# The loads of the first down products' activations move from the sync queue to GpSimd's queue

## The chip, the cores and the metric

The kernel runs on one core of a Trainium2 chip. The metric is the device time of one execution in microseconds (us). Engines are named as in the profile: PE is TensorE's matmuls, PEld its weight loads, DVE is VectorE, ACT is ScalarE, POOL is GpSimd, SP is SyncE, which here does nothing but issue DMAs.

## The reference

One step of one layer of a hybrid decoder, for 1024 prompt tokens and 8 sampled ones. A mixer (an HGRN2 and a Mamba-2 branch) comes first; the change touches only the feed-forward part at the end:

```python
h2 = _rmsnorm(x, p['norm_mlp']) * (1 + sc2) + sh2
x = x + g2 * (jnp.square(jax.nn.relu(h2 @ p['w_up'])) @ p['w_down'])
...
y_prompt = _rmsnorm(xp, norm_final)
y_sample = _rmsnorm(xs, norm_final)
```

D_MODEL is 1024 and the inner width is 4096. Everything is float32.

## The kernel before

Activations lie transposed: a **plane** is 128 channels by NT = 1032 tokens (1024 + 8). The model width is 8 planes, the inner width 32. A float32 product is made of three fp32r matmuls: every operand is split into hi (a copy rounded to fp32r, by ACT) and lo (the rest, by DVE), and the sum takes hi*lo, lo*hi and hi*hi. A block of weights is 128x1024 (512 KB); `load_w` (L46) loads it on SP (L51), makes `wh` on ACT (L53) and `wl` on DVE (L55). There are three buffers for the raw weights `wr`, and two each for `wh` and `wl`, so a load of weights waits in SP's queue until an earlier block has been split.

**Up products.** `phase_ffn` (L1137) makes 32 planes of `relu(up)^2`. They do not stay on the core: each is written to a DRAM tile `ad0` to `ad31`, in pieces, by stores in GpSimd's queue (L1148). Planes 6 to 31 come in pairs by a Strassen scheme, `strassen_pair` (L1095): seven products (1, 7, 6, 2, 5, 4, 3 in this order) of two halves q each, every one an accumulation of 12 matmuls at L1122, and 8 pieces of result per pair, each 128x258. A piece goes through one of four buffers `r`; two of the pieces are evacuated by ACT (L1151) and DVE (L1152), the other six by DVE alone (L1177, L1178), partly with sums that ACT has kept (L1111).

**Down products.** The 32 planes are read back in four chunks c of 8, by `load_split_in` (L856): a DMA from `ad` into the tile of `lo` (L862), `hi` on ACT (L863), `lo` in place on DVE (L864). For a chunk, the 8 output planes m are made one after the other from 8 activations and one block of weights `w_down`. The first of them, chunk 0 with m = 0, is made by `DenseK` (L99, matmuls at L114): it takes the activations one plane at a time as they arrive, 9 matmuls each (three spans s of 344 tokens by three products), so plane 7 can only follow planes 0 to 6. All other products (L86) take all 8 planes of a chunk in one go. Chunk 0 thus is planes 0 to 7, from `ad0` to `ad7`; chunk 1 is planes 8 to 15, from `ad8` to `ad15`, which is not needed until the 8 products of chunk 0 are done.

**What sets the order.** The order on each engine is the scheduler's, made when the kernel is built, from priorities: what stands in `high_priority(AHEAD)` is drawn forward, and that holds for the loads of weights, for the evacuations and for the loads of chunk 0. On an engine or in a DMA queue nothing overtakes: an instruction that waits holds those behind it. A load of a plane waits for its two buffers: those of planes 0 to 3 are freed by product 1 of the last Strassen pair, 4 to 7 by its product 5, those of chunk 1 by its products 4 and 3.

The lines and names used below: `wr_23450`, `wr_23582`, `wr_23674`, `wr_23766`, `wr_23858` are the first five blocks of `w_down`, called w0 to w4; the eight stores of the last pair are called s1 to s8 in their order.

Of the kernel before, what the change touches and what calls it, by code (L numbers as in the profile page):

```python
# [23 lines left out]
KD = 8  # L24
# [13 lines left out]
def cs(s):  # L38
    return slice(s * SW, (s + 1) * SW)
# [6 lines left out]
def load_w(k, src, prio=AHEAD):  # L46

    nc = k.nc
    with k.tc.high_priority(prio):
        wr = stage(k)[:, :KD * P]  # L50
        nc.sync.dma_start(wr, src)  # L51
        wh = k.wp.tile([P, KD * P], F32R, tag="wh", name="wh", bufs=2)
        nc.scalar.activation(wh, wr, AF.Copy)  # L53
        wl = k.wp.tile([P, KD * P], F32R, tag="wl", name="wl", bufs=2)
        nc.vector.tensor_tensor(wl, wr, wh.bitcast(F32), op=ALU.subtract)  # L55
    return wh, wl
# [21 lines left out]
def dense_split(k, w, X, s, evac, M=P):  # L78
    wh, wl = w
    nc = k.nc  # L80
    acc = k.ps.tile([P, 512], F32, tag="acc", name="acc", bufs=3)
    n = len(X)
    for i, (xh, xl) in enumerate(X):
        sl = slice(i * M, (i + 1) * M)
        for j, (a, b) in enumerate(((wh, xl), (wl, xh), (wh, xh))):
            last = nc.tensor.matmul(acc[:M, :SW], a[:, sl], b[:, cs(s)],  # L86
                                    start=(i == 0 and j == 0), stop=(i == n - 1 and j == 2))
    with k.tc.high_priority(AHEAD):
        evac(s, acc[:M, :SW])
    return last  # L90


def dense(k, src, X, evac):

    w = load_w(k, src)
    return [dense_split(k, w, X, s, evac) for s in range(NS)]
# [756 lines left out]
    return split_plane(k, r, tag)  # L853


def load_split_in(k, src, tag):  # L856

    nc = k.nc
    hi = k.pp.tile([P, NT], F32R, tag=tag, name="hi")
    lo = k.pp.tile([P, NT], F32R, tag=tag, name="lo")  # L860
    raw = lo.bitcast(F32)
    nc.sync.dma_start(raw, src)  # L862
    nc.scalar.activation(hi, raw, AF.Copy)  # L863
    nc.vector.tensor_tensor(lo, raw, hi.bitcast(F32), op=ALU.subtract)  # L864
    return hi, lo
# [86 lines left out]
def gated_add(k, s, dst, base, ps, gate):  # L952

    nc = k.nc
    n = SW if s < NS - 1 else SW - NB
    nc.vector.scalar_tensor_tensor(dst[:, :n], ps[:, :n], gate[:, 0:1], base[:, :n], ALU.mult, ALU.add)  # L956
    if n < SW:
        t = k.sp.tile([P, NB], F32, tag="ga", name="ga", bufs=2)
        nc.vector.tensor_tensor(t, ps[:, n:], gate[:, 1:9], op=ALU.mult)
        nc.vector.tensor_tensor(dst[:, n:], t, base[:, n:], op=ALU.add)  # L960


def sum_sq(k, acc, x, first):
    nc = k.nc
    if first:
        nc.scalar.activation(acc, x, AF.Square)
        return
    t = k.sp.tile([P, SW], F32, tag="sq", name="sq", bufs=2)
    nc.scalar.activation(t, x, AF.Square)
    nc.vector.tensor_tensor(acc, acc, t, op=ALU.add)  # L970


def rstd_model(k, acc):
    nc = k.nc
    ps = rec_ps(k, "ss")
    nc.tensor.matmul(ps[:, :SW], k.ones, acc, start=True, stop=True)
    return rstd_from(k, ps[:, :SW], SW, 1.0 / 1024)
# [45 lines left out]
def strassen_planes(k, h2, T, i):  # L1023

    nc = k.nc
    a, b = stage(k), stage(k)  # L1030
    for x, (xh, xl) in ((a, h2[i]), (b, h2[i + 4])):
        nc.vector.tensor_tensor(x, xh.bitcast(F32), xl.bitcast(F32), op=ALU.add)
    (b11, b12), (b21, b22) = [(x[:, :HN], x[:, HN:]) for x in (a, b)]

    def sub(out, x, y):
        nc.vector.tensor_tensor(out, x, y, op=ALU.subtract)
    sub(b11, b12, b11)
    sub(b12, b22, b12)
    sub(b22, b22, b11)
    sub(b21, b21, b22)  # L1040
    for x, tag, ts in ((a, "A", (1, 3)), (b, "Q3", (4, 2))):
        p = split_plane(k, x, tag, "th", "tl")
        for n, t in enumerate(ts):
            T[t].append(tuple(y[:, n * HN:(n + 1) * HN] for y in p))


def strassen_operands(h2, T):

    def quarter(r, c):
        return [tuple(p[:, c * HN:(c + 1) * HN] for p in h2[4 * r + i]) for i in range(KD // 2)]  # L1050
    return {1: quarter(0, 0), 2: quarter(1, 0), 3: quarter(1, 1), 4: T[4], 5: T[1], 6: T[2], 7: T[3]}
# [85 lines left out]
def phase_ffn(k, x1, h2):  # L1137
    nc = k.nc
    NF = 4 * KD
    up = k.i["w_up"]  # L1140
    ad = [k.dp.tile([P, NT], F32, name="ad%d" % j) for j in range(NF)]
    bufs = iter(range(1 << 20))

    def out(j, cols):
        n = next(bufs) % 4
        pool, tag = (k.sp2, "mt") if n < 2 else (k.sp, "sq")
        r = pool.tile([P, SW], F32, tag=tag, name="r", bufs=2)[:, :cols.stop - cols.start]
        return r, lambda: nc.gpsimd.dma_start(ad[j][:, cols], r)  # L1148

    def relu2(r, ps):  # L1150
        nc.scalar.activation(r, ps, AF.Relu)  # L1151
        nc.vector.tensor_tensor(r, r, r, op=ALU.mult)  # L1152

    def evac_up(j):
        def f(s, ps):
            r, store = out(j, cs(s))
            relu2(r, ps)
            store()
        return f

    ws = [load_w(k, up[j]) for j in range(2)]
    for j, s in [(j, s) for j in range(2) for s in LAST[:2]] + [(0, LAST[2]), (1, LAST[2])]:
        dense_split(k, ws[j], h2, s, evac_up(j))

    T = {n: [] for n in (1, 2, 3, 4)}
    for j in range(2, 6):
        dense(k, up[j], h2, evac_up(j))
        strassen_planes(k, h2, T, j - 2)
    X = strassen_operands(h2, T)
    for n in range(6, NF, 2):  # L1170
        def evac(m, half, q, a, ps, n=n):
            c = half * HN + q * HQ
            r, store = out(n + m, slice(c, c + HQ))
            if a is None:
                relu2(r, ps)
            else:
                nc.vector.tensor_tensor(r, a, ps, op=ALU.add)  # L1177
                nc.vector.scalar_tensor_tensor(r, r, 0.0, r, ALU.max, ALU.mult)  # L1178
            store()
        strassen_pair(k, (up[n], up[n + 1]), X, evac)  # L1180

    def add(m):
        return lambda s, ps: gated_add(k, s, x1[m][:, cs(s)], x1[m][:, cs(s)], ps, k.modT[:, 40 + m, :])

    def act(c, j):
        tag = "A" if c % 2 == 0 else "Q2" if j < 4 else "Q3"
        return load_split_in(k, ad[c * KD + j], tag)
    down = k.i["w_down"]
    aX = []
    d = DenseK(k, (down[0],), (add(0),))  # L1190
    for j in range(KD):
        with k.tc.high_priority(AHEAD):
            aX.append(act(0, j))
        d.step(*aX[j])
    for c in range(4):
        nX = []
        for m in range(KD):
            if c == 3:
                break
            if c or m:  # L1200
                dense(k, down[c * KD + m], aX, add(m))
            nX.append(act(c + 1, m))
        if c < 3:
            aX = nX
    for s in LAST:
        acc = k.sp2.tile([P, SW], F32, tag="sqa", name="sqa", bufs=1)
        for m in range(KD):
            w = load_w(k, down[3 * KD + m])
            dense_split(k, w, aX, s, add(m))
            sum_sq(k, acc, x1[m][:, cs(s)], m == 0)  # L1210
        y = rstd_model(k, acc)
        for m in range(KD):
            xx = x1[m][:, cs(s)]
            nc.vector.scalar_tensor_tensor(xx, xx, k.norm_final[:, m:m + 1], y, ALU.mult, ALU.mult)
            nc.sync.dma_start(k.o["y"][m][:, cs(s)], xx)
# [175 lines left out]
```

## Time and profile before

| | |
|---|---|
| Median of 3 runs | 2525.54 us (2525.27 to 2528.78) |
| The profiled execution's own time | 2526.23 us |
| Its span, first to last instruction | 2524.5 us |
| Around the span | 1.73 us |
| SP's queue (q1) | 279.99 MB |
| GpSimd's queue (q0) | 17.57 MB |

Times inside the execution are counted from the start of the span. The last Strassen pair's matmuls end at about 2137.4, the first down product follows at 2137.45, and the products of chunk 0 run until about 2237. In a timeline row the columns are: start, length, engine, line, operation, out<-in, shape, count of merged instructions, and in brackets the engine's idle time ahead of the row and what ended it. A row with a count above one gives the start of the first and the time to the end of the last. A row of the stretches has its bounds, its length, the busy time of each engine, the granted clock of PE, the busy share of the 16 DMA engines, and the GB/s that they moved.

### The profile page before, as it was taken

The page shows a single profiled execution, that of the slowest core. Times are in us where ns is not written, and L with a number is a line of the kernel's source. Part 1 is how long each engine was busy: PE and PEld are TensorE (multiplying, and loading weights), DVE is VectorE, ACT ScalarE, POOL GpSimd, SP SyncE. Part 2 cuts the span into 40 slices and gives each one's busy share as a digit, 9 for nine tenths or more (in the row PEclk, how much of TensorE's full clock was granted, in tenths as well). Part 3 has the DMA queues.
Part 4 walks back from the last instruction along what each step waited for, and adds up shares of the span by engine and source line. Part 5 has one row for each costly group of instructions (what it writes and reads, how often), then busy time and mean ns, then how long its engine had stood idle before and what let it go on. Part 6 is the DMA issues. An engine that isn't in the chain of part 4 may idle for free.

```text
span 2524.5 us, 47612 instructions
## 1 busy us (share of the span) xinstructions
PE 2479.3 (98%) x19822; PEld 2419.3 (96%) x19822; DVE 1755.6 (70%) x3513; ACT 1068.9 (42%) x1577; POOL 70.0 (3%) x138
## 2 busy tenths in 40 slices
PE   8999999999999999999999999999999999999998
PEld 7999999999999999999999999999999999999997
DVE  7788888888677687787887844366976666443356
ACT  4455555555444544535535533123533334221123
POOL 0000000000000000000000000000012222000000
PEclk9999999999999999999999999999999999999999
DMA  6323232223333243343343554224333325332134
GB/s 257 120 101 103 102 102 101 93 99 93 103 111 130 91 145 122 99 145 121 101 152 106 186 193 143 76 101 136 99 112 104 106 101 183 111 110 92 68 104 148
DMA packets 103256, 300.96 MB, mean 119 GB/s; under 512 B 19056, under 2 KB 26032, under 8 KB 103024
## 3 DMA queue, kind: packets, MB, share of 16 engines
q1 hardware_dynamic: 96352, 279.99, 33.3%
q0 software_dynamic: 6256, 17.57, 2.0%
q8 instruction: 156, 2.56, 0.4%
q14 instruction: 60, 0.49, 0.1%
q10 hardware_dynamic: 432, 0.35, 0.0%
HBM read 241.02 MB, written 57.10 MB: 118 GB/s over the span
## 4 chain that ended last, share of the span: by engine, by line
PE 72%; issue 11%; DVE 9%; ACT 3%; POOL 2%; DMA 2%; SPq 0%; POOLq 0%; DVEq 0%; ACTq 0%
PE acc L86 60%; POOL ad L1148 2%; PE acc L114 2%; PE y_ps L807 1%; DVE wl L55 1%; PE yi_ps L811 1%; PE kvx_ps L771 1%; DVE lv L554 1%; DVE lv L549 1%; DMA st<-sth 1%; PE xt_ps L759 1%; PE cb_ps L741 1%; ACT lv L551 1%; DVE lv L552 1%; ACT wh L53 0%
## 5 line engine op out<-in xcount | busy, mean ns | idle before, releaser
L86 PE MATMUL acc<-hl,wh 128*128 128x344 f32 x2232 | 722.4, 324 | 0.0
L86 PE MATMUL acc<-hh,wl 128*128 128x344 f32 x2232 | 721.9, 323 | 0.2 <-DVE wl L55 0.2
L86 PE MATMUL acc<-hh,wh 128*128 128x344 f32 x2232 | 716.7, 321 | 0.0
L86 PEld LDWEIGHTS acc<-hl,wh 128*128 128x128 f32 x2232 | 419.6, 188 | 3.7 <-issue 0.8
L86 PEld LDWEIGHTS acc<-hh,wl 128*128 128x128 f32 x2232 | 419.7, 188 | 3.0 <-issue 1.8
L86 PEld LDWEIGHTS acc<-hh,wh 128*128 128x128 f32 x2232 | 420.6, 188 | 1.4 <-issue 0.4
L86 PE MATMUL acc<-hi,wl 128*128 128x344 f32 x1224 | 392.4, 321 | 1.3 <-DVE wl L55 1.3
L86 PE MATMUL acc<-lo,wh 128*128 128x344 f32 x1224 | 391.7, 321 | 1.4 <-ACT wh L53 1.4
L86 PE MATMUL acc<-hi,wh 128*128 128x344 f32 x1224 | 391.1, 320 | 0.0
L53 ACT ACTIVATE wh<-wr 128x1024 fp32r<-128x1024 f32 x198 | 209.0, 1056 | 381.2 <-PE acc L86 306.0
L55 DVE TENSOR_TENSOR wl<-wr,wh 128x1024 fp32r<-128x1024 f32 x198 | 242.3, 1224 | 182.4 <-ACT wh L53 180.4
L86 PEld LDWEIGHTS acc<-lo,wh 128*128 128x128 f32 x1224 | 230.5, 188 | 2.0 <-ACT wh L53 2.0
L86 PEld LDWEIGHTS acc<-hi,wl 128*128 128x128 f32 x1224 | 230.2, 188 | 2.1 <-DVE wl L55 1.9
L86 PEld LDWEIGHTS acc<-hi,wh 128*128 128x128 f32 x1224 | 230.3, 188 | 0.2
L956 DVE SCALAR_TENSOR_TENSOR x<-acc,modT,x 128x344 f32<-128x344 f32 (+1 forms) x120 | 68.7, 572 | 189.2 <-PE acc L86 188.4
L691 DVE SCALAR_TENSOR_TENSOR cv<-raw,cst,cv 128x1024 f32<-128x1024 f32 x96 | 122.9, 1280 | 0.0
L1122 PE MATMUL b<-th,wl 128*128 128x258 f32 x416 | 117.7, 283 | 0.0
L1122 PE MATMUL b<-tl,wh 128*128 128x258 f32 x416 | 117.7, 283 | 0.0
L1122 PE MATMUL b<-th,wh 128*128 128x258 f32 x416 | 117.5, 282 | 0.0
L1148 POOL DMA_DIRECT2D ad<-r x122 | 65.8, 540 | 1468.4 <-DVE nrm_t L146 1204.2
L551 ACT ACTIVATE lv<-lv 128x1280 f32<-128x1280 f32 x48 | 61.0, 1273 | 85.7 <-DVE lv L549 83.4
L683 ACT ACTIVATE raw<-acc 128x344 f32<-128x344 f32 x96 | 42.9, 455 | 120.1 <-PE acc L86 119.3
(287 smaller groups left out, 4458.4 us busy)
## 6 DMA issues: line engine op xcount, KB each, us to landing
wr<-w_ssm SPq DMA_DIRECT2D x48, 512.0 KB
wr<-w_down SPq DMA_DIRECT2D x48, 512.0 KB
wr<-w_ada SPq DMA_DIRECT2D x36, 512.0 KB
lo<-ad SPq DMA_DIRECT2D x32, 516.0 KB
wr<-w_hg SPq DMA_DIRECT2D x32, 512.0 KB
w<-cumd SPq DMA_DIRECT2D x32, 512.0 KB
wr<-w_up SPq DMA_DIRECT2D x32, 512.0 KB
ad<-r POOLq DMA_DIRECT2D x104, 129.0 KB, 2.2
```

What stands on the lines that cost most here:

```text
L53: nc.scalar.activation(wh, wr, AF.Copy)
L55: nc.vector.tensor_tensor(wl, wr, wh.bitcast(F32), op=ALU.subtract)
L86: last = nc.tensor.matmul(acc[:M, :SW], a[:, sl], b[:, cs(s)], start=(i == 0 and j == 0), stop=(i == n - 1 and j == 2))
L114: k.nc.tensor.matmul(ac[s][:, :SW], a[:, sl], b[:, cs(s)], start=(i == 0 and j == 0), stop=(i == self.n - 1 and j == 2))
L549: nc.vector.tensor_tensor(EQ[:, :, off:off + n], b4[:, :, lo:], b4[:, :, lo - 1:lo].broadcast_to([P, nb, n]), op=ALU.subtract)
L551: nc.scalar.activation(E, E, AF.Exp)
L552: nc.vector.tensor_tensor(EK, EK, kk[:, sl], op=ALU.mult)
L683: dense(k, w, k.hX, lambda s, ps: nc.scalar.activation(raw[:, 3 + s * SW:3 + (s + 1) * SW], ps, AF.Copy))
L691: nc.vector.scalar_tensor_tensor(cv[:, :T], raw[:, j:j + T], cw[:, j:j + 1], cv[:, :T], ALU.mult, ALU.add)
L956: nc.vector.scalar_tensor_tensor(dst[:, :n], ps[:, :n], gate[:, 0:1], base[:, :n], ALU.mult, ALU.add)
L1122: nc.tensor.matmul(acc, a[:, sl], x[:, cols], start=(p in (1, 7, 2) and i == 0 and j == 0), stop=(i == KD // 2 - 1 and j == 2), skip_group ...
L1148: return r, lambda: nc.gpsimd.dma_start(ad[j][:, cols], r)
```

## The change

`load_split_in` gets a queue as an argument, and the eight loads of chunk 0 are issued by GpSimd; those of chunks 1 to 3 stay with SP.

```diff
-def load_split_in(k, src, tag):
+def load_split_in(k, src, tag, queue=None):
...
-    nc.sync.dma_start(raw, src)
+    (queue or nc.sync).dma_start(raw, src)
...
     def act(c, j):
         tag = "A" if c % 2 == 0 else "Q2" if j < 4 else "Q3"
-        return load_split_in(k, ad[c * KD + j], tag)
+
+        return load_split_in(k, ad[c * KD + j], tag, nc.gpsimd if c == 0 else None)
```

The scheduler places things anew around it, on SP, POOL, ACT and DVE. PE's order is unchanged.

SP's queue before, from the load of plane 3 to that of plane 7. The tile on the right says which plane it is: `ad3` is plane 3, `ad10` plane 10.

```order
L862 DMA lo_23502<-ad3_19627 128x1032
L51 DMA wr_23674<-w_down 128x1024
L862 DMA lo_23516<-ad4_19628 128x1032
L862 DMA lo_23762<-ad10_19634 128x1032
L862 DMA lo_23578<-ad8_19632 128x1032
L862 DMA lo_23530<-ad5_19629 128x1032
L51 DMA wr_23766<-w_down 128x1024
L51 DMA wr_23858<-w_down 128x1024
L862 DMA lo_23544<-ad6_19630 128x1032
L862 DMA lo_23670<-ad9_19633 128x1032
L862 DMA lo_23854<-ad11_19635 128x1032
L862 DMA lo_23558<-ad7_19631 128x1032
```

The same place now, from w2 (`wr_23674`) to the last load of chunk 1:

```order
L51 DMA wr_23674<-w_down 128x1024
L862 DMA lo_23762<-ad10_19634 128x1032
L862 DMA lo_24038<-ad13_19637 128x1032
L862 DMA lo_23578<-ad8_19632 128x1032
L51 DMA wr_23766<-w_down 128x1024
L862 DMA lo_23854<-ad11_19635 128x1032
L862 DMA lo_24130<-ad14_19638 128x1032
L51 DMA wr_23858<-w_down 128x1024
L862 DMA lo_23670<-ad9_19633 128x1032
L862 DMA lo_23946<-ad12_19636 128x1032
L862 DMA lo_24222<-ad15_19639 128x1032
```

Planes 0 to 7 are gone from the queue. Planes 13 and 14 of chunk 1 have moved ahead of plane 9, and all of chunk 1 still shares the queue with the weights w3 and w4.

POOL's queue at the end of the up products as it is now. The L1148 rows are the stores s2 to s8 of the last pair, which stood there before too, in the same order and with nothing between them. (The loads of planes 0 to 2 now stand ahead of s1, and s1 ahead of the first row.)

```order
L862 DMA lo_23502<-ad3_19627 128x1032
L1148 DMA ad30_19654<-r_23350 128x258
L1148 DMA ad31_19655<-r_23366 128x258
L862 DMA lo_23516<-ad4_19628 128x1032
L1148 DMA ad31_19655<-r_23382 128x258
L1148 DMA ad31_19655<-r_23398 128x258
L862 DMA lo_23530<-ad5_19629 128x1032
L1148 DMA ad31_19655<-r_23414 128x258
L1148 DMA ad30_19654<-r_23430 128x258
L1148 DMA ad30_19654<-r_23446 128x258
L862 DMA lo_23544<-ad6_19630 128x1032
L862 DMA lo_23558<-ad7_19631 128x1032
```

Each load now stands among the stores: plane 3 behind s1, plane 4 behind s3, plane 5 behind s5, planes 6 and 7 behind s8.

ACT before, from the hi of plane 4 to the hi of plane 7. The hi tiles of planes 4 to 7 are 23515, 23529, 23543 and 23557; of planes 8 to 11 23577, 23669, 23761 and 23853; of planes 12 to 15 23945, 24037, 24129 and 24221. `r_23446` is the evacuation of s8, `wh_23584` is the split of w1.

```order
L863 ACTIVATE hi_23515<-lo_23516 128x1032
L1151 ACTIVATE r_23446<-b1_23233 128x258
L53 ACTIVATE wh_23584<-wr_23582 128x1024
L863 ACTIVATE hi_23761<-lo_23762 128x1032
L863 ACTIVATE hi_23577<-lo_23578 128x1032
L863 ACTIVATE hi_23529<-lo_23530 128x1032
L863 ACTIVATE hi_23543<-lo_23544 128x1032
L863 ACTIVATE hi_23669<-lo_23670 128x1032
L863 ACTIVATE hi_23853<-lo_23854 128x1032
L863 ACTIVATE hi_23557<-lo_23558 128x1032
```

The same place now:

```order
L863 ACTIVATE hi_23515<-lo_23516 128x1032
L863 ACTIVATE hi_23761<-lo_23762 128x1032
L1151 ACTIVATE r_23446<-b1_23233 128x258
L53 ACTIVATE wh_23584<-wr_23582 128x1024
L863 ACTIVATE hi_24037<-lo_24038 128x1032
L863 ACTIVATE hi_23529<-lo_23530 128x1032
L863 ACTIVATE hi_23577<-lo_23578 128x1032
L863 ACTIVATE hi_23853<-lo_23854 128x1032
L863 ACTIVATE hi_23543<-lo_23544 128x1032
L863 ACTIVATE hi_24129<-lo_24130 128x1032
L863 ACTIVATE hi_23669<-lo_23670 128x1032
L863 ACTIVATE hi_23557<-lo_23558 128x1032
```

Ahead of the hi of plane 7 stood four planes of chunk 1 (10, 8, 9 and 11); now there are six (10, 13, 8, 11, 14 and 9). Plane 10 also stands ahead of the evacuation of s8 and of the split of w1. DVE's lo instructions (L864) follow the order of ACT's hi.

## The prediction

> **What bounds the kernel now.** I begin with the page's first rows.
>
> ```profile
> span 2524.5 us, 47612 instructions
> PE 2479.3 (98%) x19822; PEld 2419.3 (96%) x19822; DVE 1755.6 (70%) x3513; ACT 1068.9 (42%) x1577; POOL 70.0 (3%) x138
> ```
>
> PE is busy for 98% of the span, so a change in the order of loads can win only where PE stands idle or runs slowly. The change touches the seam between the up and the down products, so I read PE's waits and then its timeline there.
>
> ```profile
> PE acc L114 <- DVE lo L864: 6.6, 3, 2.9
> ```
>
> ```profile
> 2137.45 0.32 PE L114 MATMUL acc<-lo,wh 128*128 128x344 f32 x1
> ...
> 2144.36 0.32 PE L114 MATMUL acc<-hi,wh 128*128 128x344 f32 x1
> 2146.31 0.42 PE L114 MATMUL acc<-lo,wh 128*128 128x344 f32 x1 [1.62 <-DVE lo L864]
> 2147.67 0.32 PE L114 MATMUL acc<-hi,wh 128*128 128x344 f32 x1
> 2150.86 0.42 PE L114 MATMUL acc<-lo,wh 128*128 128x344 f32 x1 [2.88 <-DVE lo L864]
> 2152.22 0.41 PE L114 MATMUL acc<-hi,wh 128*128 128x344 f32 x1
> 2154.74 0.65 PE L114 MATMUL acc<-lo,wh 128*128 128x344 f32 x1 [2.11 <-DVE lo L864]
> 2157.49 0.49 PE L86 MATMUL acc<-lo,wh 128*128 128x344 f32 x1
> 2159.18 0.32 PE L86 MATMUL acc<-lo,wh 128*128 128x344 f32 x1
> ```
>
> PE waits three times, for the lo of planes 5, 6 and 7: 1.62 + 2.88 + 2.11 = 6.61 us. Planes 0 to 4 are 45 matmuls, 44 steps from 2137.45 to 2144.36, or 0.157 us each and 1.41 us for a plane. Plane 7 took 2.75 us, from 2154.74 to 2157.49, and six more slow steps follow until 2159.18: the clock, which the stretches below show at 0.82, fell after the idling. These 15 steps took 4.44 us and should have taken 15 x 0.157 = 2.36, so 2.1 us more are lost. The seam costs 6.6 + 2.1 = 8.7 us, 0.34% of the run, and that is **all that the change can win**. About 0.2%, or 5 us, is what a measurement of this kernel can tell from no change.
>
> What is late is plane 7, and the end of the chain of waits shows how:
>
> ```profile
> 2144.92 7.42 DMA lo<-ad
> 2152.34 0.02 issue
> 2152.36 1.07 ACT hi L863
> 2153.43 0.02 issue
> 2153.45 1.25 DVE lo L864
> 2154.70 0.04 issue
> 2154.74 2.94 PE acc L114 x9
> ```
>
> Its load was issued at 2144.92, took 7.42 us, and from its landing to PE it is 2.40 us. Two things made it late. The first is its place in SP's queue:
>
> ```profile
> 2126.26 0.33 SPq L51 DMA_DIRECT2D wr<-w_down  x1
> 2126.75 0.41 SPq L862 DMA_DIRECT2D lo<-ad  x1
> 2131.61 0.33 SPq L51 DMA_DIRECT2D wr<-w_down  x1
> 2132.10 5.05 SPq L862 DMA_DIRECT2D lo<-ad  x4
> 2137.24 5.93 SPq L51 DMA_DIRECT2D wr<-w_down  x2
> 2143.23 4.50 SPq L862 DMA_DIRECT2D lo<-ad  x8
> ```
>
> Read with the order of the queue, these are w1, plane 3, w2, planes 4, 10, 8, 5, then w3 and w4, and then the other eight. Of the two weights in the fifth row the second, w4, leaves only at about 2142.8 (the row ends at 2143.17, and an issue is 0.33 us), when w1 has been split, and planes 6 and 7 stand behind it. The second thing is the transfer itself:
>
> ```profile
> 2132.40:2143.00 10.60, 10.60 (x80) 10.60 (x79) 7.75 (x13) 5.54 (x8) 3.23 (x6) 1.00 0.98 346
> 2143.00:2145.00 2.00, 1.68 (x11) 1.40 (x9) 2.00 (x2) 1.53 (x2) 0.00 (x0) 1.00 0.83 218
> 2145.00:2156.40 11.40, 5.11 (x24) 4.45 (x25) 7.82 (x8) 6.38 (x6) 0.00 (x0) 0.82 1.01 403
> ```
>
> The DMA engines are full from 2132.4 to 2156.4, but for a dip to 0.83 around 2144 while SP waited to send w4.
>
> ```profile
> 2148.47 1.06 ACT L863 ACTIVATE hi<-lo 128x1032 fp32r<-128x1032 f32 x1 [3.94 <-DMA lo<-ad]
> 2149.77 1.06 ACT L863 ACTIVATE hi<-lo 128x1032 fp32r<-128x1032 f32 x1 [0.24 <-DMA lo<-ad]
> 2151.07 1.07 ACT L863 ACTIVATE hi<-lo 128x1032 fp32r<-128x1032 f32 x1 [0.23 <-DMA lo<-ad]
> 2152.36 1.06 ACT L863 ACTIVATE hi<-lo 128x1032 fp32r<-128x1032 f32 x1 [0.22 <-DMA lo<-ad]
> ```
>
> These are the hi of planes 6, 9, 11 and 7. Each waits for its DMA, and they come 1.30 us apart ((2152.36 - 2148.47) / 3). So **one load costs 1.30 us of full DMA engines**, and when plane 7 can start is a matter of counting the loads that must land before it.
>
> **The change part by part.** *The eight loads leave SP's queue.* This removes 8 issues of 0.32 to 0.41 us from SP, worth nothing by themselves, since SP only waits. It also frees planes 5, 6 and 7 of their wait behind w3 and w4. Their bytes stay, on the same 16 DMA engines.
>
> *They enter POOL's queue.* Eight issues of some 0.6 us there, against this row of a store:
>
> ```profile
> L1148 POOL DMA_DIRECT2D ad<-r x122: 539/539/551, 1812.0 to 2141.5; - x122
> ```
>
> POOL is idle most of the time, so that is hidden. What is not hidden is the order among the stores. Plane 3 stands behind s1, which left at 2128.70:
>
> ```profile
> 2128.70 0.54 POOL L1148 DMA_DIRECT2D ad<-r  x1 [7.63 <-DVE r L1178]
> 2139.38 0.54 POOL L1148 DMA_DIRECT2D ad<-r  x1 [2.54 <-DVE r L1152]
> 2141.48 0.54 POOL L1148 DMA_DIRECT2D ad<-r  x1 [1.56 <-DVE r L1152]
> ```
>
> It can go at 2129.24, where SP sent it at 2126.75: 2.5 us later. Planes 6 and 7 stand behind s7 and s8; if s8 still leaves at 2141.48 they follow at 2142.0 and 2142.6, before 2143.23 and 2144.92, some 1 to 2 us earlier than now.
>
> How long a 516 KB load takes in POOL's queue no row shows; the nearest are the stores in that queue, of 129 KB, first all 122, then the six between 2132 and 2142:
>
> ```profile
> DMA to landing us min/median/max: 2.0/2.2/7.4
> DMA to landing us min/median/max: 4.5/5.2/6.7
> ```
>
> The 387 KB more are 1 us at 403 GB/s. So a load takes from 3.0 us in a quiet stretch (2.0 + 1) to 8.4 (7.4 + 1). Planes 0 to 3 go in a stretch with gaps, and I take 4 us for them, near the quiet end; for planes 4 to 7 the queue's share of full engines is what counts, below.
>
> *The order on ACT and DVE.* This is where the gain goes. ACT does nothing out of order, and the hi of plane 7 now stands behind planes 10, 13, 8, 11, 14 and 9, where it stood behind 10, 8, 9 and 11. Plane 9 leaves SP after w4, as plane 7 did before, and w4 still waits for the split of w1, which on ACT stands behind planes 4 and 10 and the evacuation of s8. So w4 does not leave much before 2142.8, and neither does plane 9.
>
> *The count.* I count what must land from w2 on, since the DMA engines are full from there. Before, up to plane 7: w2, 4, 10, 8, 5, w3, w4, 6, 9, 11, 7, that is 11 loads. Now plane 7 needs on SP w2, 10, 13, 8, w3, 11, 14, w4, 9 and on POOL 4, 5, 6, 7, that is 13. Two more (planes 13 and 14) cost 2 x 1.30 = **+2.6 us**. The dip at 2143 should be filled, because planes 13, 11 and 14 are queued by then: 2.0 us x (1 - 218 / 403) = **-0.9 us**. If plane 9 is the last to land, its hi goes ahead of that of plane 7, one more ACT instruction of 1.06 us: **+1.1 us**. The sum is +2.8 us for the start of plane 7 on PE, at about 2157.5. PE reaches plane 7 earlier in any case: seven planes at 1.41 us from 2137.45 end at 2147.3. Until then a delay on PE of up to 10 us goes into the same wait. The slow clock behind the idling I leave as it is, at +0.
>
> The Trainium skill's page "DMA: Bandwidth & Descriptors", section "Issuing engines are not separate DMA queues", says that DMAs of all engines end on the same 16 DMA engines and that several issuers save only issue time. By that rule the change gives no bandwidth, as the busy share of 1.01 with one queue also says. Its section "Queues, rings and completion order" says that a DMA engine takes turns between queues, packet by packet. By that planes 4 to 7 would get half of the engines and land before plane 9, and the sum stays +2.8; no row here shows two long loads side by side.
>
> If instead POOL's loads come last, as the stores' 4.5 to 6.7 us under load suggest, planes 12 and 15 go in front too: 4 x 1.30 - 0.9 = +4.3 us. If the first 10.6 us ran at the 403 GB/s of the last stretch and not at 346, they would move as much in 1.5 us less, and it is +1.3. What comes behind plane 7 gives nothing back: chunk 1 is wanted 80 us later, and the split of w2 has 11 us.
>
> **The rivals.** *The change does what it says.* Planes 5 to 7 land in time, PE never waits, the clock holds: -8.7 us, 2516.8. For it speaks that planes 6 and 7 pass w4 and plane 9 in the queues. Against it, ACT's order makes plane 7 wait for plane 9 all the same, and 13 loads at 1.30 us from 2132.4 do not end before 2149, with 2.4 us to PE behind; PE would want it at 2147.3.
>
> *Nothing is won or lost.* The issue times of the last loads fall by 1 to 2 us, the dip fills, and a higher rate in the first stretch makes good the two loads: -1.5 to +1 us, 2525.3. For it speaks that 13 loads at 1.30 us from 2132.4 plus 2.4 to PE would be 2151.7 if the stores cost nothing; against it, 346 GB/s is what the stretch with stores shows.
>
> *Slower, by the stores' place.* If a load in POOL's queue takes over 4.5 us, plane 3 lands after 2133.7, and its hi ends after 2134.74:
>
> ```profile
> 2134.74 1.07 ACT L53 ACTIVATE wh<-wr 128x1024 fp32r<-128x1024 f32 x1 [1.98 <-PE b L1122]
> ```
>
> That is the split of w0, which then starts late; w3 leaves late, as it takes w0's buffer, and the same happens with plane 4, w1 and w4. At 8.4 us this is 3.9 us: w4 leaves at 2146.7, plane 9 behind it, and the dip comes back. Then 3.9 + 2.6 + 1.1 = +7.6 us, 2533.8. For it speaks that s3 to s8 needed 4.5 to 6.7 us; against it, that plane 3 goes in a quieter stretch.
>
> **How the numbers follow.** The forecast (+1.3 to +4.3, likeliest +2.8) gets 0.52, nothing won or lost 0.22, slower by the stores' place 0.19, the full gain 0.07. The sums stand against the profiled execution's 2526.23 us; the median of the three runs is 0.7 lower, 2525.54, and I predict on it: 2525.54 + 2.8 = **2528.3**. For the range I take the rival without effect, -1.5 or 2524.0, and the slow one at +7.6 with some tenths, 2533.5; the forecast alone would be 2526.8 to 2529.8. Only the full gain lies below. Faster by over 0.2% (5 us) is that case alone, 0.07. Slower by over 0.2% is the slow rival where it reaches 5 us, and a little of the forecast's tail: 0.19. Within: 0.74.
>
> **What would show it.** In the changed profile, PE's waits for lo at L114 should still be there, 7 to 12 us in all, the last for plane 7 ending between 2155 and 2160. The DMA share should be near 1 from 2132 to 2156 without the dip at 2143, w4 should leave near 2142.8, and ACT's hi of plane 7 should follow directly on that of plane 9. The split of w0 should start at 2134.7; later means the slow rival. The prediction fails to the fast side if plane 9 lands before 2147, and to the slow side if loads in POOL's queue take more than 5 us from plane 3 on.

## The result and the profile after

| | before | after |
|---|---|---|
| Median | 2527.03 us of 9 runs (2525.27 to 2531.73) | 2532.34 us of 9 runs (2530.45 to 2534.33) |
| Ratio | | 1.0020, 95% interval 1.0011 to 1.0029 |
| Profiled execution, own time and span | 2526.23 and 2524.5 us | 2530.49 and 2528.7 us |

The change makes the kernel slower by some 5.1 us (0.0020 x 2527; 2.8 to 7.3 by the interval). The page of the changed kernel first, its span and the two DMA queues (packets, MB, share):

```profile
span 2528.7 us, 47600 instructions
...
q1 hardware_dynamic: 95200, 275.76, 32.4%
q0 software_dynamic: 7408, 21.80, 2.5%
```

The change does what it says: eight loads of 0.53 MB (4.23 MB) have gone from SP's queue q1 to GpSimd's q0. PE's waits between 2100 and 2210 (line waited for: us in total, times, longest):

```profile
PE acc L114 <- DVE lo L864: 7.8, 3, 4.6
PE acc L114 <- DVE wl L55: 1.4, 1, 1.4
PE acc L114 <- ACT wh L53: 0.8, 1, 0.8
PE b L1122 <- DVE wl L1068: 0.4, 1, 0.4
```

Instead of 6.6 us there are 10.4. The three waits for lo are longer in sum, and three waits are new, all of them *ahead* of where the loads were late before: for the split of w0 (L53, L55) and even inside the last Strassen pair (L1068). So something came late early on. POOL's timeline:

```profile
2119.86 1.08 POOL L1148 DMA_DIRECT2D ad<-r  x2 [3.73 <-DVE wr L1068]
2120.93 1.59 POOL L862 DMA_DIRECT2D lo<-ad  x3
2131.63 0.55 POOL L1148 DMA_DIRECT2D ad<-r  x1 [9.11 <-PE b L1122]
2132.17 0.53 POOL L862 DMA_DIRECT2D lo<-ad  x1
...
2135.38 0.54 POOL L862 DMA_DIRECT2D lo<-ad  x1
...
2147.54 1.07 POOL L862 DMA_DIRECT2D lo<-ad  x2
```

Planes 0 to 2 leave at 2120.93, behind two stores (SP sent plane 0 at 2119.00), and s1 leaves at 2131.63, not at 2128.70. Plane 3 behind it leaves at 2132.17, planes 6 and 7 at 2147.54, behind s8. ACT's timeline, hi of planes 0 and 3, the split of w0, then hi of planes 4 and 10:

```profile
2125.76 1.07 ACT L863 ACTIVATE hi<-lo 128x1032 fp32r<-128x1032 f32 x1 [3.74 <-DMA lo<-ad]
...
2136.88 1.07 ACT L863 ACTIVATE hi<-lo 128x1032 fp32r<-128x1032 f32 x1 [5.86 <-DMA lo<-ad]
2137.86 1.04 ACT L53 ACTIVATE wh<-wr 128x1024 fp32r<-128x1024 f32 x1
...
2142.90 2.03 ACT L863 ACTIVATE hi<-lo 128x1032 fp32r<-128x1032 f32 x2 [1.84 <-DMA lo<-ad]
```

Plane 0 landed 4.8 us after its issue (2125.76 - 2120.93; 3.8 on SP before, from 2119.00 to 2122.76), so its hi is 3.0 us late, DVE's lo and the evacuation of s1 behind it are late, plane 3 is issued late, lands late, and the split of w0 starts at 2137.86 instead of 2134.74. Plane 4 stands behind s3 and leaves at 2135.38, where SP sent it at 2132.10; its hi starts at 2142.90 (2138.51 before), and on ACT the evacuation of s8 and the split of w1 stand behind it. The weights are late too, SP's rows of w3, w4 and the last planes of chunk 1:

```profile
2140.71 0.33 SPq L51 DMA_DIRECT2D wr<-w_down  x1
...
2147.88 0.33 SPq L51 DMA_DIRECT2D wr<-w_down  x1
2148.25 1.98 SPq L862 DMA_DIRECT2D lo<-ad  x3
```

w4 leaves 5.0 us later than 2142.8, when w1 has been split. The end of the chain of waits runs from plane 4's load through it:

```profile
2135.38 7.49 DMA lo<-ad
...
2142.90 1.08 ACT hi L863
...
2146.72 1.14 DVE wl L55
2147.88 0.33 SPq L51
...
2148.25 8.59 DMA lo<-ad
...
2156.87 1.07 ACT hi L863
...
2159.11 1.23 DVE lo L864
...
2160.39 1.69 PE acc L114 x9
```

The split of w0 is not on this chain: PE's waits for it end before it waits for planes 5 to 7. The last load in the chain is that of plane 9, which belongs to chunk 1 and is wanted 80 us later: its hi stands ahead of plane 7's on ACT, and plane 7 starts at 2160.39 (2154.74 before). But plane 7 itself was hardly earlier. The landings of planes 6 and 7, issued behind s8 at 2147.54 and 2148.07:

```profile
DMA to landing us min/median/max: 6.5/7.6/8.6
```

Plane 7 landed at 2156.63, 0.2 us before plane 9 (2156.84). With the 2.40 us from landing to PE that the prediction read, it could have started at 2159.03 by estimate, so of the 5.65 us plane 9's place ahead of it makes some 1.4. The three stretches of the prediction, after:

```profile
2132.40:2143.00 10.60, 8.42 (x63) 7.97 (x62) 7.13 (x13) 2.50 (x4) 4.58 (x9) 1.00 0.94 338
2143.00:2145.00 2.00, 2.00 (x15) 2.00 (x14) 1.00 (x1) 2.00 (x3) 0.00 (x0) 1.00 0.99 400
2145.00:2156.40 11.40, 4.61 (x28) 4.04 (x26) 8.62 (x10) 7.20 (x8) 1.60 (x3) 0.99 1.02 405
```

The dip around 2144 is filled (400 GB/s for 218), but the first stretch is no longer full (0.94, with PE at 8.42 of 10.6 us).

### The profile page after: what moved, and what is told of

Read it like the earlier page. It is cut to its first block, busy times and chain, and to the rows that moved or that the text cites. A ratio compares the mean times of both kernels' runs of the same rounds, so it can differ in the third digit from the quotient of the medians.

```text
span 2528.7 us, 47600 instructions
## 1 busy us (share of the span) xinstructions
PE 2481.2 (98%) x19822; PEld 2420.2 (96%) x19822; DVE 1753.9 (69%) x3513; ACT 1068.1 (42%) x1577; POOL 74.3 (3%) x146
## 4 chain that ended last, share of the span: by engine, by line
PE 71%; issue 11%; DVE 11%; ACT 3%; POOL 2%; DMA 2%; POOLq 0%; SPq 0%; DVEq 0%; ACTq 0%
PE acc L86 59%; POOL ad L1148 2%; PE acc L114 2%; PE y_ps L807 1%; DVE wl L55 1%; PE yi_ps L811 1%; PE kvx_ps L771 1%; DVE lv L554 1%; DVE lv L549 1%; DMA lo<-ad 1%; DVE lv L552 1%; DVE lv L546 1%; PE xt_ps L759 1%; ACT lv L551 1%; PE cb_ps L741 1%
## 5 line engine op out<-in xcount | busy, mean ns | idle before, releaser
L55 DVE TENSOR_TENSOR wl<-wr,wh 128x1024 fp32r<-128x1024 f32 x198 | 242.0, 1223 | 184.9 <-ACT wh L53 183.4
L53 ACT ACTIVATE wh<-wr 128x1024 fp32r<-128x1024 f32 x198 | 209.0, 1056 | 380.2 <-PE acc L86 307.6
L1148 POOL DMA_DIRECT2D ad<-r x122 | 65.9, 541 | 1471.6 <-DVE nrm_t L146 1205.1
```

## The experiments

Two theories at the start: *late splits* (the early loads in POOL's queue come late, and with them w0, w3, w1, w4 and plane 9) and *the prediction's own* (two more loads of chunk 1 and one more hi stand ahead of plane 7). The profiled executions of these runs reach the seam up to 8 us apart, so below a place in the seam is told from the first store of the last pair but one ("from the pair's store", 2108.48 before, 2108.37 after); by that clock hi of plane 0 starts at 14.28 us before and 17.39 after, and the split of w0 at 26.26 and 29.49. All ratios are against the kernel before, timed on the same chip; the places in the seam are each read from one execution.

**Planes 0 to 3 alone in GpSimd's queue.**

```diff
-        return load_split_in(k, ad[c * KD + j], tag, nc.gpsimd if c == 0 else None)
+        return load_split_in(k, ad[c * KD + j], tag, nc.gpsimd if c == 0 and j < 4 else None)
```

> Only planes 0 to 3 are loaded in GpSimd's queue; planes 4 to 7 stay with SP, and the order of ACT and of SP from w2 on is as before the change. Theory of the late splits (planes 0 to 3 land about 3 us later, hold ACT, and so delay the splits of w0 and w1 and with them w3 and w4): the split of w0 starts at about 2138 instead of 2134.7, w3 leaves at about 2140.7 instead of 2137.2, w4 at 2145 to 2147 instead of 2142.8, plane 7 starts on PE at 2157 to 2159 instead of 2154.7, and the time is 2 to 5 us above that of before. Theory of the count (what costs is only the two more loads ahead of plane 7): no load more stands ahead of plane 7 than before, so it starts at 2154.7 and the time is within 1 us of before.

Ratio 1.0012 (1.0003 to 1.0020). The split of w0 starts 29.29 us from the pair's store (2138.54 less 2109.25), as late as with the whole change.

**Planes 4 to 7 alone**, with `j >= 4` in place of `j < 4`.

> Only planes 4 to 7 are loaded in GpSimd's queue. Theory of the late splits: planes 0 to 3 land as before, the split of w0 starts at 2134.7 and w3 leaves at 2137.2; what is left is plane 4, which ACT meets ahead of the split of w1, so w4 leaves at 2143 to 2146; the time is 0 to 3 us above before. Theory of the count: one more load than before (plane 13) stands ahead of plane 9 on SP and ACT, so plane 7 starts 1.3 to 2.4 us later than 2154.7, and the time is 1 to 3 us above before. Theory of the slow queue (long loads in GpSimd's queue take 7 to 11 us beside full engines, whatever else is done): planes 4 to 7 land 7 to 11 us after their issue, and the time is 3 to 7 us above before.

Ratio 1.0008 (0.9999 to 1.0016). The split of w0 is where it was (26.25), PE waits 6.8 us, and plane 7 starts on PE 1.4 us later than before (47.62 from the pair's store, 46.26 before). That and the time are what the prediction's own theory gives here, and the late splits allow them too, so this run does not separate the two. The ratios of the two halves overlap; by the start of plane 7 (49.19 with planes 0 to 3 alone) more of the loss goes with the early planes.

**The change, with chunk 1's hi behind plane 7's.** `k.ld` holds the load and the hi of the plane last loaded, `last` those of plane 7; `order` only tells the scheduler which stands first.

```diff
             nX.append(act(c + 1, m))
+            if c == 0:
+                order(k, k.ld[1], last[1])
```

> The change as it is, but on ACT (and so on DVE) every plane of chunk 1 comes behind plane 7; SP's queue is nearly as in the change. Theory of the order on ACT (plane 7 waits for planes 10, 13, 8, 11, 14 and 9): w4 leaves about 2 us earlier than in the change, since the split of w1 no longer waits for plane 10, and plane 7 goes to PE 2.4 us after its own landing, at 2153 to 2157 instead of 2160.4; the time is 3 to 7 us below the change, near before. Theory of the slow queue: planes 6 and 7 land 8 us or more after an issue at 2145 or later, plane 7 starts at 2156 or later, and at most 3 us of the change's loss come back. In both the split of w0 stays late, at about 2138.

Ratio 1.0014 (1.0005 to 1.0022). PE's waits for lo fall from 7.8 us to 3.8, and plane 7 starts 2.5 us earlier than with the change (49.52 for 52.02), but the waits for w0's split stay, and the split is no earlier (29.97). At the seam ACT's order is part of the delay, not its origin. Of the 3 to 7 us that I expected from it the ratios show 1.5, which they cannot tell from nothing.

**The kernel before, with chunk 1's loads and hi behind plane 7's.** The queue is SP for all planes, and both orders are set:

```diff
+            if c == 0:
+                order(k, k.ld[0], last[0])
+                order(k, k.ld[1], last[1])
```

> The kernel before the change (all loads on SP), but chunk 1 is ordered behind plane 7 in SP's queue and on ACT and DVE. If it was chunk 1's loads ahead of planes 5 to 7 that made PE wait before, the queue alone was not at fault: planes 4, 5, 6 and 7 stand behind w2, w2, w3 and w4, plane 7 leaves SP just behind w4 (2141 to 2143), lands 4 to 5 us later and starts on PE at 2148 to 2150; PE's waits at L114 fall from 6.6 us to 3 or less, and the time is 4 to 8.7 us below before. If full DMA engines were the limit by themselves, little would be won: 0 to 2 us.

Ratio 0.9985 (0.9976 to 0.9993), faster than both kernels by this ratio; 3.8 us is a little less than I expected. One wait is left between 2100 and 2400:

```profile
PE acc L114 <- DVE lo L864: 3.5, 1, 3.5
```

**Planes 3 to 7 in GpSimd's queue**, `j >= 3`. The whole change but for three planes.

> Planes 3 to 7 in GpSimd's queue, planes 0 to 2 in SyncE's as before. Asked: does plane 3 come late because its own load is in GpSimd's queue, or because planes 0 to 2 there make the store s1, behind which plane 3's issue stands, late? If s1 does it: s1 leaves POOL at about 2128.7 us as before (2131.6 with the change), plane 3 is issued at 2129.2, lands within 4.7 us at 2134, the split of w0 starts at 2134.5 to 2136 instead of 2137.9, and the time is between that of the kernel with only planes 4 to 7 moved and that with planes 0 to 3 moved, +1.0 to +2.5 us. If the load in that queue is slow by itself: the split of w0 starts at 2137 or later and the time is +3 us or more.

Ratio 1.0003 (0.9994 to 1.0012). POOL's rows of s1 and plane 3, then ACT's hi of plane 0 and of plane 3 and the split of w0, of an execution that comes 4.35 us later to the seam:

```profile
2133.04 0.54 POOL L1148 DMA_DIRECT2D ad<-r  x1 [7.64 <-DVE r L1178]
2133.57 0.54 POOL L862 DMA_DIRECT2D lo<-ad  x1
```

```profile
2127.00 1.07 ACT L863 ACTIVATE hi<-lo 128x1032 fp32r<-128x1032 f32 x1 [0.52 <-DMA lo<-ad]
...
2137.96 1.07 ACT L863 ACTIVATE hi<-lo 128x1032 fp32r<-128x1032 f32 x1 [3.99 <-DMA lo<-ad]
2139.09 1.06 ACT L53 ACTIVATE wh<-wr 128x1024 fp32r<-128x1024 f32 x1
```

Less 4.35, s1 leaves at 2128.69 and the split of w0 starts at 2134.74, both as before, although plane 3 is in GpSimd's queue and behind s1. So it is planes 0 to 2 that make s1 and plane 3 late. The run also shows what planes 3 to 7 do to the end of the seam. Here is the stretch from the same place to plane 7 on PE, in the kernel before and in this one, and below them ACT's hi of planes 6 and 7 in this one:

```profile
2132.40:2154.74 22.34, 15.73 (x107) 14.79 (x105) 15.94 (x20) 12.39 (x14) 3.23 (x6) 0.95 0.98 360
```

```profile
2136.75:2160.28 23.53, 16.79 (x107) 15.67 (x105) 17.08 (x20) 13.95 (x15) 4.82 (x9) 0.95 0.97 380
```

```profile
2155.35 2.02 ACT L863 ACTIVATE hi<-lo 128x1032 fp32r<-128x1032 f32 x2 [1.31 <-DMA lo<-ad]
2157.90 1.06 ACT L863 ACTIVATE hi<-lo 128x1032 fp32r<-128x1032 f32 x1 [0.54 <-DMA lo<-ad]
```

The engines move 380 GB/s for 360, and still plane 7 starts 1.2 us *later* (23.53 us for 22.34). Its own load, issued at 2148.22, landed 9.7 us later, and its hi at 2157.90 waited for that and not for a plane of chunk 1. Between the hi of planes 6 and 7 stands only one plane here (the second of the row at 2155.35), where the change has planes 14 and 9. So this is not the prediction's count of 13 loads, but at least one load less.

**Planes 0 to 2 alone**, `j < 3`.

> Planes 0 to 2 alone in GpSimd's queue, planes 3 to 7 in SyncE's as before. If s1 and plane 3 behind it carry the loss: s1 is late as with the change (about 2131.6 us instead of 2128.7), but plane 3 no longer stands behind it (SyncE issues it near 2126.8), so the split of w0 starts at 2134.5 to 2135.5 and the time is -0.5 to +1 us. If late planes 0 to 2 are enough, by the Strassen product's own splits on ScalarE and VectorE: the split of w0 starts at 2136.5 or later and the time is +2 us or more.

Ratio 1.0013 (1.0004 to 1.0022), some 3.3 us: three loads alone lose most of it. They lie ahead of the Strassen pair's own splits on ACT and DVE, and SP's first row here (w0 and w1) shows what follows:

```profile
2110.17 19.89 SPq L51 DMA_DIRECT2D wr<-w_down  x2
2130.22 0.33 SPq L862 DMA_DIRECT2D lo<-ad  x1
```

w1 leaves at 2129.7 and not at 2126.26, since the buffer it takes is split late, and plane 3 waits behind it, now on SP: 2130.22 and not the 2126.8 that I expected. The split of w0 starts 1.4 us late (27.68 from the pair's store), between what the two sides of my expectation said, while the time falls on the second.

**The kernel before, with w4 and chunk 1 behind plane 7.** As the run with chunk 1 behind, and the load of w4 (`k.wld`) is ordered behind plane 7's too:

```diff
                 dense(k, down[c * KD + m], aX, add(m))
+                if c == 0 and m == 4:
+                    order(k, k.wld, last[0])
```

> The queue of before, chunk 1's load and hi ordered behind those of plane 7, and also the load of w4 ordered behind plane 7's on SyncE. If the order in the queue and on ScalarE is the whole bound: plane 7 is issued 4 to 5 us earlier than 2143.8, TensorE's one remaining wait for lo (3.5 us) goes, the first product behind the seam starts at 2149 to 2150 us, and the time is -6 to -8 us. If the DMA engines' bytes bound the seam: the loads take that much longer, the wait remains at 2 us or more, and the time is -3 to -5 us, as without w4's move.

Median 2520.31 us, ratio 0.9968 (0.9956 to 0.9981): 8.1 us faster than before (4.8 to 11.1), and the lowest ratio of all. PE hardly waits:

```profile
PE acc L114 <- DVE lo L864: 0.4, 1, 0.4
```

The first product behind the seam starts at 2149.51 (2157.49 before), inside the first theory's 2149 to 2150.

**The kernel before, with w4 alone behind plane 7.**

> The kernel before with one thing alone: the load of w4 ordered behind plane 7's on SyncE; chunk 1's loads and hi's stay where the scheduler has them. If a plane's place in SyncE's queue behind w4 (which waits for the split of w1 on ScalarE) makes it late: the loads of planes 6 and 7 leave 3 to 5 us earlier, TensorE waits 2 to 4 us less, and the time is -1.5 to -4 us. If ScalarE's order (hi of planes 8 and 9 ahead of those of 5 to 7) is what holds: the waits at the first down product stay within 1 us of 6.6 us and the time is within 1 us of before.

Ratio 0.9989 (0.9981 to 0.9998). PE's waits fall by 1.7 us, to 4.9. Either order alone wins a part. By PE's waits (4.9, 3.5 and 0.4 us) it takes both to win all; the intervals of the three ratios touch.

**The two stores ahead of plane 0 moved to SP**, first with planes 0 to 2 in GpSimd's queue, then with the whole change:

```diff
-        return r, lambda: nc.gpsimd.dma_start(ad[j][:, cols], r)
+        return r, lambda q=nc.gpsimd: q.dma_start(ad[j][:, cols], r)
...
-            store()
+            store(nc.sync if n == NF - 4 and a is None else nc.gpsimd)
```

> Planes 0 to 2 alone in GpSimd's queue, as before this run, but the two stores ahead of them there (at 2119.9 us) go to SyncE's queue. Asked: of the 3.1 us by which hi of plane 0 came late, how much is the place behind the two stores (plane 0 issued at 2120.97 instead of 2119.00) and how much the load in that queue (4.8 us instead of 3.7)? If both as read: plane 0 is issued near 2119.0, lands at 2123 to 2124, hi of plane 0 starts there (2126.2 with the stores ahead, 2122.8 before), s1 leaves at 2129 to 2130, and the seam loses 0 to 0.8 us instead of 1.8. If the stores' place does not matter (POOL would have issued late anyway, or the load lands at 2126 whatever its issue): hi of plane 0 at 2125.5 or later and the loss stays at 1.5 us or more.

> The whole change, with the two stores ahead of plane 0 (at 2119.86 us) in SyncE's queue. If the loss of the change starts at planes 0 to 2, and planes 3 to 7 in GpSimd's queue cost nothing by themselves: s1 leaves POOL by 2129 to 2130 instead of 2131.6, plane 3 is issued right behind it, the split of w0 starts at 2134.7 to 2136, and the seam is 0 to 1.5 us later than before instead of 4.0, time 0 to +2 us. If the loads' slowness in that queue beside full DMA engines carries it: the seam stays 3 us or more later, time +3 to +6 us.

Ratios 1.0011 (1.0002 to 1.0020) and 1.0015 (1.0006 to 1.0024): no better, against my theory. POOL's rows of the first, the store ahead and then planes 0 to 2, and below them the semaphore waits of these loads (count, min/median/max in ns, first and last start):

```profile
2117.39 0.54 POOL L1148 DMA_DIRECT2D ad<-r  x1 [0.90 <-DVE r L1178]
2123.80 1.60 POOL L862 DMA_DIRECT2D lo<-ad  x3 [5.87 <-PE b L1122]
```

```profile
L862 POOLq EVENT_SEMAPHORE  x3: 43/43/3319, 2117.4 to 2124.3; - x3
```

The wait of plane 0 ended at 2120.7 (2117.4 + 3.32), 10.5 us from the pair's store, exactly where SP sent it before (10.52). Yet POOL issues it only at 2123.80, 3.1 us later, with nothing to wait for. The stores were held in the same way. Before the change, a pair's seventh and eighth store two pairs ahead, and in the last pair but one:

```profile
2076.95 0.54 POOL L1148 DMA_DIRECT2D ad<-r  x1 [1.13 <-DVE r L1152]
2078.49 0.54 POOL L1148 DMA_DIRECT2D ad<-r  x1 [1.00 <-DVE r L1152]
...
2119.99 1.08 POOL L1148 DMA_DIRECT2D ad<-r  x2 [3.74 <-DVE wr L1068]
```

```profile
2116.66 0.42 DVE L1152 TENSOR_TENSOR r<-r 128x258 f32<-128x258 f32 x1
```

The value of the seventh store was ready at 2117.08, and it left 2.91 us later, where in the pairs ahead, with the same DVE instructions beside it, it takes 0.3 us. In the kernel before, the change and these two runs the held instruction is POOL's 115th DMA, counted along the trace, and in all four it is also the same instruction by number (the 249th, as I counted in the programs).

**The change with 16 more small memsets on POOL at the start.**

```diff
-    for t in k.qz:
+    for t in k.qz * 9:
         nc.gpsimd.memset(t, 0.0)
```

> The whole change, with 16 more small memsets on POOL at the program's start, so that every later POOL instruction stands 16 places later. The runs so far have one odd hold on POOL: the store that is its 115th DMA (its 249th instruction) leaves 2.9 us after what it waits for (119.99 for 117.08, of 2100), before and after the change; with the two stores moved away, plane 0's load is the 249th instruction and is itself held (2122.1 by the clock of before, 2119.0 on SyncE). If the hold belongs to the instruction's place: it falls some 8 DMAs earlier, on a store that nobody waits for, the two stores leave at about 2117.4 and 2118.9, plane 0 is issued at 2119.0 to 2119.5 and lands 4.8 us later, so that hi of plane 0 starts at 2123.8 to 2124.3 (2125.76 with the change, 2122.76 before), s1 leaves near 2130, and the seam is 1.5 to 3 us later than before instead of 4.0. If the hold belongs to the DMA's count or to this place of the program: the two stores leave at 2119.9 again, hi of plane 0 starts at 2125.5 or later, and the seam is 3.5 to 4.5 us later.

Ratio 1.0025 (1.0015 to 1.0036). The same stores are held (11.50 us from the pair's store, as before): it is not the instruction's place.

**The change with the 16 gate stores of earlier phases in GpSimd's queue.**

```diff
-    nc.sync.dma_start(k.gd[n], t[:, :NT])
+    nc.gpsimd.dma_start(k.gd[n], t[:, :NT])
```

> The whole change, with the 16 gate stores of the earlier phases (SyncE's before, long before the seam) in GpSimd's queue too, so that the same store is POOL's 131st DMA instead of its 115th. The 16 more instructions did not move the hold of 2.9 us on that store. If it belongs to the count of DMAs (or of what they put into the queue): it falls 16 or more DMAs earlier, on a store that nobody waits for; of the last pair but one, the seventh and eighth store leave 0.3 us after their values are ready, 1.5 us apart; plane 0 is issued 10.5 to 10.9 us after that pair's first store (12.56 with the change, 10.52 before on SyncE) and hi of plane 0 starts 15.2 to 15.8 us after it (17.39; 14.28), and the seam is 1.5 to 3 us later than before instead of 4.0. If it belongs to this place of the program: the two stores leave together 11.5 us after the first, and the seam is 3.5 to 4.5 us later. The earlier phases may shift by the moved stores, so the seam is read against that pair's first store, and the whole time says little.

POOL's rows of the seventh and eighth store two pairs ahead of the last pair but one, then of the eighth store of the last pair but one and of planes 0 to 2:

```profile
2084.58 1.08 POOL L1148 DMA_DIRECT2D ad<-r  x2 [3.73 <-DVE wr L1068]
...
2123.95 0.54 POOL L1148 DMA_DIRECT2D ad<-r  x1 [1.00 <-PE b L1122]
2124.54 1.62 POOL L862 DMA_DIRECT2D lo<-ad  x3
```

The hold has moved by exactly 16 stores, to two pairs earlier: it goes with the count of POOL's DMAs, whatever their size. Plane 0 now leaves 11.03 us from the pair's store (12.56 with the change, 10.52 before), its load still takes 4.9 us, and its hi starts at 15.92 (17.39 and 14.28). So of the 3.1 us by which hi of plane 0 was late, the hold made 1.5; 0.5 of issue and 1.1 of a slower load remain. The split of w0 is 1.6 us earlier than with the change (27.93), but PE's waits are 9.9 us (10.4), plane 7 starts where it did (52.00 for 52.02), and the ratio is 1.0017 (1.0007 to 1.0027): the end of the seam won nothing that can be measured. Its chain of waits is the same; w4 leaves 0.8 us earlier (38.68 for 39.51), but plane 9's load behind it takes 9.4 us and not 8.6.

All runs side by side, in us from the pair's store, with PE's waits at the seam:

| Kernel | hi of plane 0 | split of w0 | plane 7 on PE | split of w4 | PE waits | ratio |
|---|---|---|---|---|---|---|
| before | 14.28 | 26.26 | 46.26 | 72.67 | 6.6 | |
| the change | 17.39 | 29.49 | 52.02 | 76.67 | 10.4 | 1.0020 |
| planes 0 to 3 | 17.21 | 29.29 | 49.19 | 75.64 | 7.6 | 1.0012 |
| planes 0 to 2 | 17.82 | 27.68 | 49.69 | 74.48 | 8.1 | 1.0013 |
| planes 4 to 7 | 14.56 | 26.25 | 47.62 | 74.09 | 6.8 | 1.0008 |
| planes 3 to 7 | 14.17 | 26.26 | 47.46 | 72.42 | 6.7 | 1.0003 |
| planes 0 to 2, two stores on SP | 17.92 | 27.61 | 49.11 | 76.04 | 7.4 | 1.0011 |
| the change, two stores on SP | 18.17 | 30.33 | 52.08 | 77.55 | 8.9 | 1.0015 |
| the change, 16 memsets | 17.75 | 30.03 | 52.55 | 79.02 | 9.3 | 1.0025 |
| the change, gate stores | 15.92 | 27.93 | 52.00 | 79.20 | 9.9 | 1.0017 |
| the change, hi of chunk 1 behind | 17.87 | 29.97 | 49.52 | 75.05 | 6.5 | 1.0014 |
| before, w4 behind | 14.22 | 26.25 | 45.74 | 72.71 | 4.9 | 0.9989 |
| before, chunk 1 behind | 14.36 | 26.26 | 42.94 | 67.73 | 3.5 | 0.9985 |
| before, both behind | 14.36 | 26.26 | 39.82 | 64.15 | 0.4 | 0.9968 |

The split of w4 is good to about 2 us only. The change and the change with 16 memsets start plane 7 0.5 us apart, yet the latter comes out 2.35 us behind the former at the split of w4, with *less* waiting. Most of the difference is the clock that PE is granted in the 10 us in which plane 7 starts (from 50.00 us behind the pair's store):

```profile
2158.37:2168.37 10.00, 9.05 (x53) 8.39 (x53) 7.65 (x11) 3.49 (x4) 0.00 (x0) 0.94 0.17 53
```

```profile
2155.84:2165.84 10.00, 9.04 (x40) 8.60 (x40) 7.76 (x10) 4.01 (x5) 0.00 (x0) 0.65 0.12 38
```

With PE busy for 9.0 us in both, 53 matmuls were begun with a granted clock of 0.94 (after the change), 40 with 0.65 (with the memsets). The 13 that are missing are 2.0 us by estimate, at the 0.157 us of a full-clock step.

## Why the prediction was right in its sign and wrong in its size

The forecast was 2528.3 us, or +2.8, in a range that reached 2533.5. Measured is +5.1 by the ratio (2.8 to 7.3), at the 0.2% that I took as measurable, where I had put most of the chance (0.74) below it. The measured 2532.3 us lie inside the range, but it reached that far only for the slow rival; the forecast alone ended at 2529.8. So the sign is owed to the mechanism, but that the range held is owed to a rival with a chance of 0.19 and not to the sum, and is in part luck. (Of the 4.0 us between 2528.3 and 2532.3, 1.5 are the base: nine runs of the kernel before have a median of 2527.03, not 2525.54.)

- **All that can be won is 8.7 us: right.** Both orders set on the kernel before win 8.1 us and leave 0.4 us of waiting.
- **Nothing is gained because plane 7 stays behind plane 9, and plane 9 behind w4: right.** The chain of waits shows it after the change, and taking these places away on SP wins what the queue did not. It is not all, though: plane 7's own load left late too, and landed only 0.2 us before plane 9.
- **The dip is filled: right**, at 400 GB/s.
- **The count, +2.6: not settled.** With planes 4 to 7 moved one load more stands ahead of plane 7, which starts 1.4 us later; with planes 3 to 7 moved it starts 1.2 us later, with plane 9 no longer ahead of it. Both are near the 1.30 us of one load, so they speak for a price per load. No run has all 13 loads with planes 0 to 2 on time. The 346 GB/s of the first stretch, which were taken to stay, were 338 with the change and 378 with planes 3 to 7 (from 2136.75 to 2147.35).
- **"Planes 0 to 3 go in a stretch with gaps, and I take 4 us": wrong, and the step that failed**, since the sum puts nothing for planes 0 to 2. Plane 0 took 4.8 us and left 1.9 us later, behind two stores that I did not count and of which the first was held for 2.9 us. I asked only what stands ahead of planes 3, 6 and 7. With planes 0 to 2 moved besides 3 to 7, plane 7 starts at 52.02 from the pair's store, without them at 47.46: 4.6 of the 5.8 us by which it is late.
- **A load in POOL's queue takes 3.0 to 8.4 us: too little at the top.** Planes 4 to 7 took 7.5, 10.7, 6.5 and 8.6 us, and over 5 us was the prediction's own sign of the slow side.
- **"It can go at 2129.24" (plane 3): wrong for the same reason.** I took s1's 2128.70 as given. But s1's evacuation on DVE stands behind lo of planes 0 and 1, so the moved loads delay the store that the next moved load stands behind: 2131.63.
- **"If s8 still leaves at 2141.48", and "w4 does not leave much before 2142.8": s8 left at 2147.01 and w4 at 2147.88.** Both stand on ACT behind the hi of plane 4, whose load waited behind the late s3. Planes 6 and 7 left 5.5 us later than the 2142.0 and 2142.6 of the prediction.
- **Slower by the stores' place, 0.19: this is what happened**, with another way in. I let it hang on plane 3's load alone (over 4.5 us); that load took 4.7 us, hardly over, and with planes 3 to 7 moved it made nothing late. The split of w0 was 3.1 us late all the same, because of planes 0 to 2, and w4 5.0 us late. The +7.6 of this rival was too much: it took 8.4 us for plane 3's load and let the dip come back.

How the 5 us divide is shown in part: planes 0 to 2 alone cost 3.3 us (1.0 to 5.6) and planes 3 to 7 alone 0.8 (-1.5 to 3.0). What the hold is worth in time is not settled: without it half of the early delay is gone, but neither the late start of plane 7 nor the loss.

## What to carry to other kernels

When a load moves into another engine's queue, look up for the *first* of the moved loads what stands ahead of it there and what stands behind its consumer on every engine, since a late first load delays the very stores that the next ones queue behind. Before moving transfers to another queue, try their order in the old one: here chunk 1's loads, and one block of weights, stood ahead of the planes that PE waited for, and two orders won 8 us where the second queue lost 5.

## What the runs showed of the hardware that I had not expected

- POOL's 115th DMA is held for 2.9 to 3.1 us after its waits have ended, be it a store of 129 KB or a load of 516 KB. 16 more DMAs ahead moved it by 16 DMAs, 16 more memsets did not move it. What it is, no run tells.
- A load of 516 KB in GpSimd's queue lands 4.3 to 5.3 us after its issue where only two more such loads follow it (plane 0 in all runs that moved it; 3.8 on SP), and up to 11.1 us beside full engines (plane 5 with chunk 1's hi behind). The Trainium skill's page "DMA: Bandwidth & Descriptors", section "Anatomy of one DMA — SWDGE (gpsimd) path", gives 2.0 us and the bytes at 436 GB/s, by estimate 3.2 us; the traces do not agree.
- The clock granted to PE behind the same seam of the same instructions was 0.94 in one execution and 0.65 in another, and the second came out 2.35 us later with 1.1 us less of waiting. What brings the lower clock on, no run here separates.
